# One encoder layer in float32 on one core: residual scaling on VectorE, FFN operands made operand by operand, FFN2's first casts moved

## The chip, the cores and the metric

The kernel runs on one core of one Trainium2 chip. The metric is device time in microseconds (us), the median of several runs. A profiled execution has a time of its own, and inside it a span from the first to the last instruction, in which all times of the trace are counted.

## The reference, cut to what matters

The model is a single encoder layer that is applied to a prompt of 512 tokens and to a sample of 256 tokens, each with the same 16 meta tokens in front. The width is 1024, all in float32.

```python
h   = layer_norm(concat(meta, x), ln_in_g, ln_in_b)
mix = concat(mla_attention(h), bidirectional_gated_delta_net(h)) @ w_out   # 8 heads each
h   = layer_norm(ALPHA * h + mix, ln1_g, ln1_b)
ff  = square(relu(h @ w_ff1)) @ w_ff2                                      # 1024 -> 4096 -> 1024
h   = layer_norm(ALPHA * h + ff, ln2_g, ln2_b)                             # meta tokens are dropped
```

The 768 real tokens are handled as six blocks of 128, in the order `TO = (4, 5, 1, 2, 0, 3)`. The first three blocks are "half 0" of the FFN's tokens and the last three are "half 1".

## The kernel before, in words

Each product of float32 matrices is made from three products. `split` (lines 210 to 213) rounds an operand to a short form on ScalarE (a cast, line 212) and takes the remainder on VectorE (a subtraction, line 213). TensorE then multiplies high by high, high by low and low by high.

The stages follow each other. The first layer norm and the projections (line 331) come first, up to about 270 us in the trace. The gated delta net then runs as a chain of small matrix steps (lines 837 to 882), and the attention is laid beside it: `scores` makes the softmax of one head (lines 954 to 987), `values` multiplies it with the value rows (989 to 1005). Behind them come the residual (1036 to 1049), the output projection in two passes (the loop at 1096), FFN1 (1147 to 1222) and FFN2 (1225 to 1295). The program is written in one order, but a planner with a simulated clock sets the order on each engine. From then on every engine works its queue strictly in that order. The manual dependencies marked `NOSYNC` are hints to the planner only, and nothing waits for them on the chip.

The residual. `acc` holds the six blocks of the normalized input. Each block is loaded again from `x` (1045) and normalized on ScalarE (1047). It is then multiplied by the gain row on GpSimd (1048), and the bias row is added on VectorE (1049). The two rows lie in `rbs` (1040 to 1042), in a pool that is opened after the memory of the delta net is given back. The load of block `ti` is placed behind the values of head `ti`.

The output projection. Pass 0 multiplies the delta net's output and pass 1 the attention's. Each pass loads four strips of `w_out` (1101), splits them, and makes 12 groups of 12 matmuls (1129). A group is drained into `acc` by VectorE (1131 or 1133). Pass 1 then normalizes the block (1136, 1137). After the third block it makes the transposed half 0 of the FFN's input (1138 to 1141).

FFN1 works on 2 by 2 blocks by Strassen and Winograd's scheme with seven products instead of eight. `pair(m)` computes two of the 32 strips of 128 FFN columns for both token halves. Its seven products (`prod`, 12 matmuls of 384 columns each) take the token operands B11, T2, B21, T1, T3, B22 and T4, in this order. B11 and B21 are half 0 itself. The others are sums of half 0 (kept as `raw0` in the first 3072 columns of the big tile `LT`) and half 1, made in the loop at 1152 to 1163. The sums of weights are made inside `pair`. The first two products of pairs 0 and 1 are made early (`ahead`, lines 1113 to 1117 and 1142 to 1144), into all four PSUM banks named `w`. The result `fo_` of a pair lies in `LT` where `raw0` lay. It is squared on ScalarE (1208, 1209) and stored to `FD`.

FFN2 loads the squares of a pair (`f_load`, 1235) and one strip of `w_ff2` (`w2_load`, 1242), splits both, and adds 18 matmuls (1275) for each of the 32 strips to six PSUM banks. This is done for half 0 and then for half 1. In its third step the second layer norm's gain and bias are put on `acc` by twelve VectorE operations (1263).

Of the kernel before, what the change touches and what calls it, by code (L numbers as in the profile page):

```python
# [5 lines left out]
F32 = mybir.dt.float32  # L6
# [7 lines left out]
P = 128  # L14
# [123 lines left out]
def body(ctx, tc, I, O):  # L138
# [898 lines left out]
    ex = ExitStack()  # L1037
    op = pool(ex, "op", 1)
    os_ = pool(ex, "os", 2)
    rbs = [os_.tile([P, D], F32, name="rb") for i in range(2)]  # L1040
    for i in range(2):
        ld(rbs[i], I["rows"][i].partition_broadcast(P))
# [11 lines left out]

    def w1_raw(m):

        o = 3 * D + m % 2 * 2 * D
        wr = LTf[:, o:o + 2 * D].rearrange("p (q k c) -> p q k c", q=4, k=HQ)
        ld(wr[:, 0:2], I["w_ff1"][m].rearrange("p (q k) c -> p q k c", q=2))
        ld(wr[:, 2:4], I["w_ff1"][m + 16].rearrange("p (q k) c -> p q k c", q=2))  # L1060
        return wr
# [3 lines left out]
        split(src, wh, wl)  # L1065
        return wh, wl

    def prod(w, n, ps=None):
        ps = ps if ps is not None else nbank()
        (wh, wl), (bh, bl) = w, fq[n]  # L1070
        for k in range(HQ):
            for i, (a, b) in enumerate(((wh, bh), (wh, bl), (wl, bh))):
                T.matmul(ps[:, :HR], lhsT=a[:, k, :], rhs=b[:, k, :],  # L1073
                         start=(k == 0 and i == 0), stop=(k == HQ - 1 and i == 2))
        return ps[:, :HR]

    nb = [0]
# [18 lines left out]
    for half in range(2):  # L1096
        wo = []
        for k in range(4):
            wr = op.tile([P, D], F32, name="wor", bufs=2)
            r0 = (1 - half) * 512 + k * P  # L1100
            ld(wr, I["w_out"][r0:r0 + P, :])
            wo.append([op.tile([P, D], F32R, name=n, bufs=5) for n in ("woh", "wol")])
            split(wr, *wo[k])
        if half == 1:
            banks_set(w=4, b=4)
            e5.close()
            eh = ExitStack()
# [5 lines left out]
            ahead = {}  # L1113
            for m in range(2):
                wr = LTf[:, 6 * D:7 * D].rearrange("p (q k c) -> p q k c", q=2, k=HQ)
                ld(wr, I["w_ff1"][m].rearrange("p (q k) c -> p q k c", q=2))
                ahead[m] = [w1_split(wr[:, i]) for i in range(2)]
        src = (Oa, mf)[half]
        for ti, t in enumerate(TO):
            qs = slice(t * P, t * P + P)  # L1120
            a = acc[:, ti]
            mh, ml_ = (os_.tile([P, 4, P], F32R, name=n) for n in ("mh", "ml"))
            split(src[:, :, qs], mh, ml_)
            for s in range(2):
                cs = slice(s * 512, s * 512 + 512)
                ps = bank()
                for k in range(4):
                    for i, (x, y) in enumerate(((mh, wo[k][0]), (mh, wo[k][1]), (ml_, wo[k][0]))):
                        T.matmul(ps, lhsT=x[:, k, :], rhs=y[:, cs], start=(k == 0 and i == 0), stop=(k == 3 and i == 2))  # L1129
# [19 lines left out]
    for n in ("T2", "T1", "T3", "B22", "T4"):  # L1149
        fq[n] = [hq.tile([P, HQ, HR], F32R, name=n + x) for x in "hl"]  # L1150
    fu = pool(eq, "fu", 2)
    for k in range(HQ):
# [12 lines left out]
    FD = dp.tile([16, P, 4, HR], F32, name="FD")  # L1165

    def pair(m):

        wr = w1_raw(m)
# [7 lines left out]
        sm1 = fv.tile([P, 2, HQ, P], F32, name="s12", bufs=2)  # L1177
        i1 = V.tensor_add(sm1[:, 0], wr[:, 2], wr[:, 3])
        if m in ahead:
            tc.add_manual_dep(i1.ins, normed.ins.name, NOSYNC, reason="behind the norms")  # L1180
        V.tensor_sub(sm1[:, 1], sm1[:, 0], wr[:, 0])
        p6 = prod(w1_split(sm1[:, 1]), "T2")
# [7 lines left out]
        p5 = prod(w1_split(sm1[:, 0]), "T1")  # L1190
        u4 = fu.tile([P, HR], F32, name="p5s")
        V.tensor_add(u4, u2, p5)
        yield
        V.tensor_sub(wr[:, 2], wr[:, 0], wr[:, 2])
        p7 = prod(w1_split(wr[:, 2]), "T3")
# [4 lines left out]
        V.tensor_sub(wr[:, 1], wr[:, 1], sm1[:, 1])  # L1200
        p3 = prod(w1_split(wr[:, 1]), "B22")
        V.tensor_add(fo_[:, 1], u4, p3)
        yield
        p4 = prod(w1_split(wr[:, 3]), "T4")
# [5 lines left out]
        st(FD[m], fo_)  # L1210

    for m in range(14):
        for _ in pair(m):
# [26 lines left out]
        return f[:, 0], f[:, 1]  # L1240

    def w2_load(n, ft):
        o = (3 + n % 4) * D
        wr = LTf[:, o:o + D]
        ld(wr, I["w_ff2"][ft * P:(ft + 1) * P, :])
        w = fw.tile([P, 2, D], F32R, name="w2h", bufs=7)
        return split(wr, w[:, 0], w[:, 1]), w[:, 0], w[:, 1]

    rb2 = None
    seq = [(m, i) for m in range(16) for i in range(2)]  # L1250
    for s in range(2):
# [2 lines left out]
        last = []  # L1254
        for n, (m, i) in enumerate(seq):
            if i == 0:
                fh, fl = f_load(s, m)
            x, wh, wl = w2_load(n, m + 16 * i)
            if s == 0 and n == 2:
                rb2 = rows2(2)  # L1260
                for ti in range(6):
                    for j, fn in enumerate((V.tensor_mul, V.tensor_add)):
                        y = fn(acc[:, ti], acc[:, ti], rb2[:, j])
                        tc.add_manual_dep(y.ins, x.ins.name, NOSYNC, reason="not before it is needed")
                rb2 = rows2(4)
# [46 lines left out]
```

## Time and profile before

| what | value |
|---|---|
| time, median of 3 runs | 1221.97 us (1216.72 to 1222.62) |
| the profiled execution, its own time | 1223.56 us |
| its span | 1221.8 us |
| TensorE matmuls, busy share of the span | 92% |
| VectorE, busy share | 68% |
| ScalarE, busy share | 49% |
| GpSimd, busy share | 14% |
| mean granted TensorE clock | 0.959 of full |

TensorE has the largest share by far, so the time that can be won lies where TensorE stands still or runs at a lower clock. The profile names an engine's idle time together with the instruction that ended it. The granted clock is 1.00 at 2.4 GHz and 0.50 at 1.2 GHz, and a figure between the two is a stretch that has some of each.

### The profile page before, as it was taken

What the parts mean: (1) busy time and instruction counts of PE and PEld (TensorE: products, weight loads), DVE (VectorE), ACT (ScalarE), POOL (GpSimd) and SP (SyncE); (2) the same over time, 40 slices, a digit from 0 to 9 for tenths busy, and PEclk for the clock granted to TensorE, in tenths of its full rate; (3) what the DMA queues carried; (4) which work ended last, traced back from release to release, by engine and by line L of the source; (5) the groups of instructions that cost most, each with busy time, mean ns of one, the idle gap of its engine ahead of it and who ended that gap; (6) DMA issues with size and microseconds to landing.
All of it is one profiled execution on the core that took longest, in us unless ns stands there. A gap on an engine that the chain in (4) does not pass through costs nothing.

```text
span 1221.8 us, 18631 instructions
## 1 busy us (share of the span) xinstructions
PE 1129.0 (92%) x7116; PEld 976.4 (80%) x7116; DVE 835.5 (68%) x1352; ACT 594.8 (49%) x1054; POOL 171.7 (14%) x201
## 2 busy tenths in 40 slices
PE   5978989998999999996898979999997999999997
PEld 4867879998899876663576769999997788888886
DVE  8557668688876877679646698677675844494446
ACT  5574655234745667563424566545554333333330
POOL 2144553014322211004000000000000000000000
PEclk9988899999999999897999889999999899999999
DMA  5157765532388755324102024333325765556531
GB/s 205 52 118 178 186 168 134 124 102 78 121 273 229 223 144 145 88 69 139 60 18 73 32 69 168 133 121 121 122 112 178 260 221 167 183 196 216 165 104 52
DMA packets 108107, 169.47 MB, mean 139 GB/s; under 512 B 36258, under 2 KB 72866, under 8 KB 108018
## 3 DMA queue, kind: packets, MB, share of 16 engines
q1 hardware_dynamic: 108018, 168.28, 45.0%
q8 instruction: 56, 0.92, 0.3%
q14 instruction: 33, 0.27, 0.1%
HBM read 129.14 MB, written 39.11 MB: 138 GB/s over the span
## 4 chain that ended last, share of the span: by engine, by line
PE 72%; DVE 14%; DMA 6%; issue 3%; ACT 3%; POOL 1%; SPq 1%; DVEq 0%; ACTq 0%; POOLq 0%
PE w L1275 14%; PE w L1073 9%; PE b L1073 8%; PE b L1275 7%; PE d L331 7%; PE b L1129 5%; DMA x<-gD 4%; PE c L1003 3%; PE d L972 3%; PE d L704 2%; PE b L837 2%; PE b L853 2%; PE b L877 2%; PE b L870 2%; DVE LP L598 2%
## 5 line engine op out<-in xcount | busy, mean ns | idle before, releaser
L1275 PE MATMUL w<-w2h,fh 128*128 128x512 f32 x768 | 186.9, 394 | 9.0 <-ACT fh L212 6.5
L1275 PEld LDWEIGHTS w<-w2h,fh 128*128 128x128 f32 x768 | 146.0, 190 | 40.2 <-ACT fh L212 6.8
L331 PE MATMUL d<-hTh,wl 128*128 128x384 f32 (+1 forms) x352 | 123.9, 352 | 4.4 <-DVE wl L213 4.4
L331 PE MATMUL d<-hTh,wh 128*128 128x384 f32 (+1 forms) x352 | 124.7, 354 | 1.4 <-ACT ks L188 1.4
L331 PE MATMUL d<-hTl,wh 128*128 128x384 f32 (+1 forms) x352 | 124.6, 354 | 0.0
L213 DVE TENSOR_TENSOR w2h<-LT,w2h 128x1024 fp32r<-128x1024 f32 x64 | 77.8, 1224 | 52.2 <-ACT w2h L212 50.0
L212 ACT CAST w2h<-LT 128x1024 fp32r<-128x1024 f32 x64 | 66.7, 1049 | 69.4 <-PE w L1275 27.1
L1275 PE MATMUL b<-w2h,fh 128*128 128x512 f32 x384 | 97.4, 392 | 0.0
L1275 PEld LDWEIGHTS b<-w2h,fh 128*128 128x128 f32 x384 | 72.9, 190 | 15.3
L212 ACT CAST w1h<-LT 128x512 fp32r<-128x512 f32 x80 | 49.0, 616 | 52.7 <-PE w L1073 22.6
L331 PEld LDWEIGHTS d<-hTh,wl 128*128 128x128 f32 x352 | 67.4, 192 | 6.8 <-DVE wl L213 4.7
L331 PEld LDWEIGHTS d<-hTh,wh 128*128 128x128 f32 x352 | 67.4, 191 | 5.7 <-issue 2.8
L213 DVE TENSOR_TENSOR fh<-fr,fh 128x768 fp32r<-128x768 f32 x32 | 30.5, 957 | 59.7 <-ACT fh L212 59.7
L331 PEld LDWEIGHTS d<-hTl,wh 128*128 128x128 f32 x352 | 67.3, 191 | 2.1 <-issue 1.5
L212 ACT CAST fh<-fr 128x768 fp32r<-128x768 f32 x32 | 26.7, 838 | 75.9 <-PE w L1275 38.7
L213 DVE TENSOR_TENSOR w1l<-LT,w1h 128x512 fp32r<-128x512 f32 x80 | 55.0, 688 | 5.6 <-ACT w1h L212 5.3
L1208 ACT ACTIVATE LT<-LT 128x384 f32<-128x384 f32 (+1 forms) x32 | 27.1, 846 | 46.6 <-DVE LT L1205 37.4
L972 PE MATMUL d<-kt,q 128*128 128x512 f32 (+1 forms) x96 | 46.0, 584 | 2.2 <-ACT p L188 1.3
L1003 PE MATMUL c<-pt,vt 128*64 128x512 f32 (+3 forms) x96 | 42.0, 536 | 2.6 <-ACT pt L1002 1.6
L1129 PE MATMUL b<-woh,mh 128*128 128x512 f32 x96 | 41.1, 438 | 2.3 <-DVE acc L1131 1.0
L1129 PE MATMUL b<-wol,mh 128*128 128x512 f32 x96 | 39.7, 414 | 2.4 <-DVE wol L213 2.3
L857 DVE TENSOR_TENSOR YZ<-U,b 64x512 f32<-64x512 f32 x52 | 35.5, 683 | 8.1 <-PE b L853 7.6
(455 smaller groups left out, 2789.6 us busy)
## 6 DMA issues: line engine op xcount, KB each, us to landing
LT<-in_w_ff SPq DMA_DIRECT2D x98, 512.0 KB, 4.2
FD<-LT SPq DMA_DIRECT2D x16, 768.0 KB, 3.2
fr<-FD SPq DMA_DIRECT2D x32, 384.0 KB, 3.5
wr<-in_w_in SPq DMA_DIRECT2D x22, 512.0 KB, 3.4
x<-gD SPq DMA_DIRECT2D x16, 560.0 KB, 6.0
KV<-vD SPq DMA_DIRECT2D x26, 256.0 KB, 4.3
U<-UD SPq DMA_DIRECT2D x26, 256.0 KB, 4.6
UD<-ua SPq DMA_DIRECT2D x16, 256.0 KB, 5.2
```

The lines of the kernel that those rows point to most:

```text
L212: S.copy(hi, src)
L213: return (eng or V).tensor_sub(lo, src, hi.bitcast(F32))
L331: T.matmul(ps[:, s, :c1 - c0], lhsT=a[:, k, :], rhs=b[:, k, c0:c1], start=(k == 0 and i == 0), stop=(k == KT - 1 and i == 2))
L598: V.tensor_add(Lq[:, :, i + 1:32, 0:i], Lq[:, :, i + 1:32, 0:i], tv)
L704: T.matmul(ps[:, s, :HR], lhsT=a[:, k], rhs=b[:, cs], start=(k == 0 and i == 0), stop=(k == 2 and i == 2))
L857: V.tensor_sub(YZ[h][rows], U[rows, :, :, 0], wv[rows])
L972: T.matmul(ps[:, :w], lhsT=q[:, qs], rhs=kt[:, k0:k0 + w], start=True, stop=True)
L1003: T.matmul(po[:m, :nq], lhsT=Vs[j][:, t0 + bi, :m], rhs=pt[:, :nq], start=(bi == 0), stop=(bi == ntl - 1))
L1073: T.matmul(ps[:, :HR], lhsT=a[:, k, :], rhs=b[:, k, :], start=(k == 0 and i == 0), stop=(k == HQ - 1 and i == 2))
L1129: T.matmul(ps, lhsT=x[:, k, :], rhs=y[:, cs], start=(k == 0 and i == 0), stop=(k == 3 and i == 2))
L1208: S.activation(f, f, AF.Relu)
L1275: T.matmul(po[g][h], lhsT=a[:, i_, qs], rhs=b[:, cs], start=(n_ == 0 and j == 0), stop=(n_ == len(seq) - 1 and j == 2))
```

## The change

The diff has four parts. The two rows of the residual get a pool of their own that is opened in front of the attention, the multiplication goes from GpSimd to VectorE, and the load of each block is placed one head later. The weights of pair 0 get a tile of their own (`w1x`), and all their sums and splits are made during the projection's second pass; the raw weights of FFN1 now rotate over three places. The products made ahead are placed behind the last matmul of the projection, and the token operands are made one operand after the other (T2 for all four strips, then T1, T3, B22 and T4), with sums in place in `raw0`. The last squares of pairs 14 and 15 are placed behind FFN2's first two `f_load` and first four `w2_load`, and the twelve operations on `acc` are spread over steps 8 to 13 of FFN2.

```diff
     acc = rest.tile([P, 6, D], F32, name="acc")
+    er = ExitStack()
+    rbp = pool(er, "rbp", 1, "left")
+    rbs = [rbp.tile([P, D], F32, name=f"rb{i}") for i in range(2)]
+    for i in range(2):
+        ld(rbs[i], I["rows"][i].partition_broadcast(P))
...
-        tc.add_manual_dep(i.ins, after[(0, 1, 2, 3, 4, 5)[ti]].ins.name, NOSYNC, reason="not before it is needed")
+        tc.add_manual_dep(i.ins, after[ti + 1].ins.name, NOSYNC, reason="not before it is needed")
         S.activation(a, a, AF.Identity, bias=stat[:, 1 + t, 0:1], scale=stat[:, 1 + t, 1:2])
-        G.tensor_mul(a, a, rbs[0])
+        V.tensor_mul(a, a, rbs[0])
         V.tensor_add(a, a, rbs[1])
...
-        o = 3 * D + m % 2 * 2 * D
-        wr = LTf[:, o:o + 2 * D].rearrange("p (q k c) -> p q k c", q=4, k=HQ)
+        wr = w1x if m % 3 == 0 else LTf[:, 7 * D - m % 3 * 2 * D:9 * D - m % 3 * 2 * D]
+        wr = wr.rearrange("p (q k c) -> p q k c", q=4, k=HQ)
...
+    def w1_sums(wr):
+        s12 = fv.tile([P, 2, HQ, P], F32, name="s12", bufs=2)
+        i1 = V.tensor_add(s12[:, 0], wr[:, 2], wr[:, 3])
+        V.tensor_sub(s12[:, 1], s12[:, 0], wr[:, 0])
+        V.tensor_sub(wr[:, 2], wr[:, 0], wr[:, 2])
+        V.tensor_sub(wr[:, 1], wr[:, 1], s12[:, 1])
+        return s12, i1
...
-            for m in range(2):
-                wr = LTf[:, 6 * D:7 * D].rearrange("p (q k c) -> p q k c", q=2, k=HQ)
-                ld(wr, I["w_ff1"][m].rearrange("p (q k) c -> p q k c", q=2))
-                ahead[m] = [w1_split(wr[:, i]) for i in range(2)]
+            w1x = fv.tile([P, 2 * D], F32, name="w1x", bufs=1)
+            wr0 = w1_raw(0)
+            ahead = {0: [w1_split(wr0[:, i]) for i in range(2)]}
+            wr = LTf[:, 6 * D:7 * D].rearrange("p (q k c) -> p q k c", q=2, k=HQ)
+            ld(wr, I["w_ff1"][1].rearrange("p (q k) c -> p q k c", q=2))
+            ahead[1] = [w1_split(wr[:, i]) for i in range(2)]
+            sums0 = w1_sums(wr0)
+            early = [w1_split(x) for x in (sums0[0][:, 1], sums0[0][:, 0], wr0[:, 2], wr0[:, 1], wr0[:, 3])]
...
-                        w[:] = [prod(x, n, bank("w")) for x, n in zip(w, ("B11", "B21"))]
+                        w[:] = [prod(x, n, bank("w"), outp) for x, n in zip(w, ("B11", "B21"))]
...
     for k in range(HQ):
-        b12, b22 = (h1_full(1, k + HQ * i, fu.tile([P, HR], F32, name=n)) for i, n in enumerate(("p5s", "b22")))
-        split(b22, *(x[:, k] for x in fq["B22"]))
-        t1, t2 = (fu.tile([P, HR], F32, name=n) for n in ("u2", "u3"))
-        V.tensor_sub(t1, b12, raw0(k))
-        V.tensor_sub(b12, b22, b12)
-        V.tensor_sub(t2, b22, t1)
+        ...
+        h1_full(1, k, b12)
+        h1_full(1, k + HQ, b22)
+        V.tensor_sub(raw0(k), b12, raw0(k))
+        V.tensor_sub(t2, b22, raw0(k))
         split(t2, *(x[:, k] for x in fq["T2"]))
-        split(t1, *(x[:, k] for x in fq["T1"]))
-        split(b12, *(x[:, k] for x in fq["T3"]))
-        V.tensor_sub(t2, t2, raw0(k + HQ))
-        split(t2, *(x[:, k] for x in fq["T4"]))
+    for k in range(HQ):
+        split(raw0(k), *(x[:, k] for x in fq["T1"]))
+    for k in range(HQ):
+        V.tensor_sub(b12s[k], b22s[k], b12s[k])
+        split(b12s[k], *(x[:, k] for x in fq["T3"]))
+    for k in range(HQ):
+        split(b22s[k], *(x[:, k] for x in fq["B22"]))
+    for k in range(HQ):
+        V.tensor_sub(t2s[k], t2s[k], raw0(k + HQ))
+        split(t2s[k], *(x[:, k] for x in fq["T4"]))
...
-        for q in ((0, 1), (1, 4)):
-            f = fo_[:, q[0]:q[1]]
-            S.activation(f, f, AF.Relu)
-            S.activation(f, f, AF.Square)
+        act2(fo_[:, 0:1])
+        yield
+        act2(fo_[:, 1:4])
         st(FD[m], fo_)
...
-        o = (3 + n % 4) * D
+        o = (5, 6, 3, 4)[n % 4] * D
...
+    first = [f_load(0, 0), f_load(0, 1)]
+    firstw = [w2_load(n, n // 2 + 16 * (n % 2)) for n in range(4)]
+    behind[0] = firstw[3][0]
+    for g_ in two:
+        next(g_, None)
...
-            if s == 0 and n == 2:
-                rb2 = rows2(2)
-                for ti in range(6):
-                    for j, fn in enumerate((V.tensor_mul, V.tensor_add)):
-                        y = fn(acc[:, ti], acc[:, ti], rb2[:, j])
+            if s == 0 and 8 <= n < 14:
+                if n == 8:
+                    rb2 = rows2(2)
+                for j, fn in enumerate((V.tensor_mul, V.tensor_add)):
+                    y = fn(acc[:, n - 8], acc[:, n - 8], rb2[:, j])
```

## Rows read from the trace of the kernel before

**Rows 1.** Busy time by stretch: start:end, length, then each engine; granted clock, DMA.

```profile
500.00:548.00 48.00, 46.49 (x332) 31.38 (x332) 32.34 (x83) 27.95 (x68) 0.35 (x1) 0.93 0.23 72
...
552.00:570.00 18.00, 13.57 (x36) 8.04 (x36) 17.90 (x17) 4.64 (x7) 12.89 (x5) 0.55 0.30 109
...
939.00:960.80 21.80, 12.76 (x39) 9.74 (x38) 20.29 (x19) 13.48 (x14) 0.00 (x0) 0.77 0.68 241
690.60:735.00 44.40, 34.67 (x188) 32.05 (x187) 43.31 (x86) 28.58 (x57) 0.00 (x0) 0.92 0.17 55
548.00:600.00 52.00, 38.72 (x134) 24.30 (x133) 45.39 (x68) 21.94 (x48) 15.43 (x6) 0.80 0.36 122
```

**Rows 2.** The chain of waits: start us, us, what held it.

```profile
547.94 3.83 DMA rb<-in_rows
...
551.84 2.64 POOL acc L1048
...
554.52 3.39 DVE acc L1049
...
675.80 0.69 PE w L1073
...
681.42 1.06 PE w L1073 x6
...
973.02 2.72 PE w L1275 x12
```

**Rows 3.** TensorE in order of time, where it had stood idle.

```profile
552.42 2.05 PE L896 MATMUL b<-sq,cst 128*128 128x512 f32 x2 [3.20 <-DVE sq L893]
...
707.13 0.69 PE L1073 MATMUL w<-T2h,w1h 128*128 128x384 f32 x1 [3.33 <-ACT T2h L212]
...
945.71 3.78 PE L1275 MATMUL w<-w2h,fh 128*128 128x512 f32 x8 [6.52 <-ACT fh L212]
```

**Rows 4.** ScalarE in order of time.

```profile
704.95 0.48 ACT L1175 COPY LT<-w 128x384 f32<-128x384 f32 x1
...
937.74 1.17 ACT L1208 ACTIVATE LT<-LT 128x1152 f32<-128x1152 f32 x1 [13.47 <-DVE LT L1205]
```

**Rows 5.** GpSimd and VectorE in order of time: start us, us, instruction [idle before].

```profile
551.84 13.05 POOL L1048 TENSOR_TENSOR acc<-acc,rb 128x1024 f32<-128x1024 f32 x5 [51.49 <-DMA rb<-in_rows]
...
552.19 2.40 DVE L979 SCALAR_TENSOR_TENSOR LT<-sm__5648,mx 128x96 f32<-128x96 f32 x1
...
560.40 6.09 DVE L985 TENSOR_SCALAR p<-p,rs 128x512 f32<-128x512 f32 x6
...
566.58 1.21 DVE L1049 TENSOR_TENSOR acc<-acc,rb 128x1024 f32<-128x1024 f32 x1
...
585.28 0.26 DVE L979 SCALAR_TENSOR_TENSOR LT<-sm__5783,mx 128x96 f32<-128x96 f32 x1
...
609.17 2.20 DVE L985 TENSOR_SCALAR p<-p,rs 128x512 f32<-128x512 f32 x6
```

**Rows 6.** SyncE's queue of transfers in order of time.

```profile
568.96 14.42 SPq L1101 DMA_DIRECT2D wor<-in_w_out  x5
...
624.20 16.65 SPq L1116 DMA_DIRECT2D LT<-in_w_ff  x2
...
915.45 6.59 SPq L1245 DMA_DIRECT2D LT<-in_w_ff  x4
922.09 2.76 SPq L1237 DMA_DIRECT2D fr<-FD  x2
```

**Rows 7.** Line 1047 on ScalarE: its idle time until the block's load had landed (us, times).

```profile
  DMA acc<-in_x: 7.3, 4
```

**Rows 8.** The page's costliest groups: busy, mean ns of one | idle before them.

```profile
L212 ACT CAST w2h<-LT 128x1024 fp32r<-128x1024 f32 x64 | 66.7, 1049 | 69.4 <-PE w L1275 27.1
...
L212 ACT CAST fh<-fr 128x768 fp32r<-128x768 f32 x32 | 26.7, 838 | 75.9 <-PE w L1275 38.7
L213 DVE TENSOR_TENSOR w1l<-LT,w1h 128x512 fp32r<-128x512 f32 x80 | 55.0, 688 | 5.6 <-ACT w1h L212 5.3
```

More of the change, by code (lines that the diff above doesn't have):

```diff
@@ L1039, in body @@
     os_ = pool(ex, "os", 2)
-    rbs = [os_.tile([P, D], F32, name="rb") for i in range(2)]
-    for i in range(2):
-        ld(rbs[i], I["rows"][i].partition_broadcast(P))
     for ti, t in enumerate(TO):
@@ L1066, in w1_split, with prod @@
         return wh, wl
-    def prod(w, n, ps=None):
+    def w1_sums(wr):
[5 more added lines that the diff above has]
+        return s12, i1
+    def prod(w, n, ps=None, behind=None):
         ps = ps if ps is not None else nbank()
@@ L1072, in prod @@
             for i, (a, b) in enumerate(((wh, bh), (wh, bl), (wl, bh))):
-                T.matmul(ps[:, :HR], lhsT=a[:, k, :], rhs=b[:, k, :],
-                         start=(k == 0 and i == 0), stop=(k == HQ - 1 and i == 2))
+                x = T.matmul(ps[:, :HR], lhsT=a[:, k, :], rhs=b[:, k, :],
+                             start=(k == 0 and i == 0), stop=(k == HQ - 1 and i == 2))
+                if behind is not None and k == 0 and i == 0:
+                    tc.add_manual_dep(x.ins, behind.ins.name, NOSYNC, reason="behind the projection")
         return ps[:, :HR]
@@ L1106, in body @@
             e5.close()
+            er.close()
             eh = ExitStack()
@@ L1112, in body @@
             fv = pool(ef, "fv", 2, "left")
-            ahead = {}
-            for m in range(2):
-                wr = LTf[:, 6 * D:7 * D].rearrange("p (q k c) -> p q k c", q=2, k=HQ)
-                ld(wr, I["w_ff1"][m].rearrange("p (q k) c -> p q k c", q=2))
-                ahead[m] = [w1_split(wr[:, i]) for i in range(2)]
+            w1x = fv.tile([P, 2 * D], F32, name="w1x", bufs=1)
[6 more added lines that the diff above has]
+            early = [w1_split(x) for x in (sums0[0][:, 1], sums0[0][:, 0], wr0[:, 2], wr0[:, 1], wr0[:, 3])]
         src = (Oa, mf)[half]
@@ L1128, in body @@
                     for i, (x, y) in enumerate(((mh, wo[k][0]), (mh, wo[k][1]), (ml_, wo[k][0]))):
-                        T.matmul(ps, lhsT=x[:, k, :], rhs=y[:, cs], start=(k == 0 and i == 0), stop=(k == 3 and i == 2))
+                        outp = T.matmul(ps, lhsT=x[:, k, :], rhs=y[:, cs], start=(k == 0 and i == 0), stop=(k == 3 and i == 2))
                 if half == 0:
@@ L1176, in pair @@
         yield
[L1177 to L1182, printed above, removed]
+        if m == 0:
+            w6, w5, w7, w3, w4 = early
+        else:
+            s12 = fv.tile([P, 2, HQ, P], F32, name="s12", bufs=2)
+            V.tensor_add(s12[:, 0], wr[:, 2], wr[:, 3])
+            V.tensor_sub(s12[:, 1], s12[:, 0], wr[:, 0])
+            w6 = w1_split(s12[:, 1])
+        p6 = prod(w6, "T2")
         u2 = fu.tile([P, HR], F32, name="u2")
@@ L1189, in pair @@
         yield
-        p5 = prod(w1_split(sm1[:, 0]), "T1")
+        if m:
+            w5 = w1_split(s12[:, 0])
+        p5 = prod(w5, "T1")
         u4 = fu.tile([P, HR], F32, name="p5s")
@@ L1193, in pair @@
         yield
-        V.tensor_sub(wr[:, 2], wr[:, 0], wr[:, 2])
-        p7 = prod(w1_split(wr[:, 2]), "T3")
+        if m:
+            V.tensor_sub(wr[:, 2], wr[:, 0], wr[:, 2])
+            w7 = w1_split(wr[:, 2])
+        p7 = prod(w7, "T3")
         u3 = fu.tile([P, HR], F32, name="u3")
@@ L1199, in pair, with act2 @@
         yield
-        V.tensor_sub(wr[:, 1], wr[:, 1], sm1[:, 1])
-        p3 = prod(w1_split(wr[:, 1]), "B22")
+        if m:
+            V.tensor_sub(wr[:, 1], wr[:, 1], s12[:, 1])
+            w3 = w1_split(wr[:, 1])
+        p3 = prod(w3, "B22")
         V.tensor_add(fo_[:, 1], u4, p3)
         yield
-        p4 = prod(w1_split(wr[:, 3]), "T4")
+        if m:
+            w4 = w1_split(wr[:, 3])
+        p4 = prod(w4, "T4")
         V.tensor_sub(fo_[:, 2], u3, p4)
-        for q in ((0, 1), (1, 4)):
-            f = fo_[:, q[0]:q[1]]
-            S.activation(f, f, AF.Relu)
-            S.activation(f, f, AF.Square)
+        act2(fo_[:, 0:1])
+        yield
+        act2(fo_[:, 1:4])
         st(FD[m], fo_)
+    behind = [None]
+    def act2(f):
+        x = S.activation(f, f, AF.Relu)
+        if behind[0] is not None:
+            tc.add_manual_dep(x.ins, behind[0].ins.name, NOSYNC, reason="behind the first casts")
+        S.activation(f, f, AF.Square)
     for m in range(14):
@@ L1256, in body @@
             if i == 0:
-                fh, fl = f_load(s, m)
-            x, wh, wl = w2_load(n, m + 16 * i)
-            if s == 0 and n == 2:
-                rb2 = rows2(2)
-                for ti in range(6):
-                    for j, fn in enumerate((V.tensor_mul, V.tensor_add)):
-                        y = fn(acc[:, ti], acc[:, ti], rb2[:, j])
-                        tc.add_manual_dep(y.ins, x.ins.name, NOSYNC, reason="not before it is needed")
-                rb2 = rows2(4)
+                fh, fl = first[m] if s == 0 and m < 2 else f_load(s, m)
+            x, wh, wl = firstw[n] if s == 0 and n < 4 else w2_load(n, m + 16 * i)
+            if s == 0 and 8 <= n < 14:
[3 more added lines that the diff above has]
+                    y = fn(acc[:, n - 8], acc[:, n - 8], rb2[:, j])
+                    tc.add_manual_dep(y.ins, x.ins.name, NOSYNC, reason="not before it is needed")
+                if n == 13:
+                    rb2 = rows2(4)
             last.append((n, i, fh, fl, wh, wl))
```

9 lines of the change are left out of this document (8 added, 1 removed).

## The prediction

> **What bounds the kernel now.** I read the page's busy shares first. TensorE is busy for 92% of the span, so no other engine can be the bound as a whole, and what can be won are the stretches in which TensorE stands still or runs at its lower clock. I then cut the span into stretches of 50 us with the view of busy time by stretch, looked for low TensorE time and low granted clock, and cut finer around the three places that the diff touches. The reader is to see two columns in [rows 1]: TensorE's busy time against the length, and the clock. Where TensorE is busy at the 1.2 GHz level, half of that busy time is lost as well.
>
> The three losses are these. From 548 to 600 TensorE is busy 38.7 of 52.0 us, so 13.3 are idle; from 552 to 570 the granted clock is 0.55, so about 90% of that stretch is at the lower level, and of 13.6 us of matmuls about 6.1 are lost [rows 1]. That makes 19.4 us. From 690.6 to 735.0 it is idle for 9.7 us, and a clock of 0.92 (16% at the lower level) costs 34.7 x 0.16 / 2 = 2.8; that makes 12.5 us. From 939.0 to 960.8 TensorE does 36 matmuls of FFN2 (the other three of 39 end FFN1), which cost 0.227 us each in the steady state (2.72 us for 12) [rows 2], so 8.2 us of work take 21.8 and 13.6 us are lost. The three add up to 45.5 us; no more than that is at stake.
>
> Then I asked who holds TensorE in each place, with the chain of waits and the engines in order of time. In the first, the chain goes from the gain rows' load (3.83 us) to the first GpSimd multiplication (2.64) and to VectorE's addition (3.39) [rows 2]. In the second, VectorE is busy for 43.3 of 44.4 us [rows 1] and TensorE waits 3.33 us for T2 [rows 3]. In the third, ScalarE had been idle for 13.47 us before it squared the last pairs [rows 4], and TensorE waited 6.52 us for a cast that stood behind the squares [rows 3].
>
> **Part 1, the residual.** Removed are six GpSimd multiplications; five of them run from 551.8 to 564.9 [rows 5]. While they run, VectorE's instructions are stretched: a 128x96 operation takes 2.40 us where the same line takes 0.26 later, six softmax scalings take 6.09 where they take 2.20 later, and the first addition takes 3.39 [rows 2] where a later one takes 1.21 [rows 5]. These alone are 2.1 + 3.9 + 2.2 = 8.2 us. Behind them in VectorE's queue stand the remainders of `w_out`, and the two raw buffers of `w_out` come free only with them, so five loads are spread over 14.42 us [rows 6] and the projection can't fill TensorE's idle time. With the rows in a pool that is free before the attention, the wait for their load goes too.
>
> Added are six multiplications on VectorE at the 1.21 us of the addition, which has the same shape and operands [rows 5], 7.3 us. Four blocks should now be finished under the delta net, so eight VectorE instructions or 9.7 us come into a stretch where TensorE is busy 46.5 of 48 us and VectorE 32.3 [rows 1]. The cover is VectorE's idle 15.7 us; if none of it fits, the 9.7 show in full, and since less is queued later it could also be below nothing. I take 2. There is a new wait: the multiplication waits for ScalarE, which waited 7.3 us in four times for the block's load [rows 7]. Behind it in VectorE's queue stand the drains of the delta net and the attention, and TensorE waits for those. This is priced among the rivals.
>
> What is late next in 548 to 600: the 3.2 us for the delta net's last norm [rows 3] stay, and the projection has a single PSUM bank there, so a group's drain is not hidden behind the next group. I let 13 of the 19.4 us come back. Part 1 is worth -13 + 2 = **-11** (between -19.4 and, with nothing won and 9.7 lost, +9.7).
>
> **Parts 2 and 3, FFN1's start.** The products made ahead stood in the middle of the projection with 0.69 and 1.06 us [rows 2]. Moved behind it, they let the last block be normalized 1.7 us earlier, and they cover that norm. Four sums and five remainders of pair 0 (nine VectorE instructions at 0.69 [rows 8], 6.2 us) and five casts leave the stretch from 690.6, which VectorE fills. Its subtractions and remainders for the token operands stay the same in number; only T2 comes first. So I expect 6.2 + 1.7 = 7.9 us less, minus about 0.4 for what stays late: T4 is now the last operand, and VectorE still sets when it comes.
>
> The price is paid in the projection's second pass, where those nine instructions and five casts now stand among the splits of `w_out`, and SyncE's queue, which was already held for 16.65 us by two loads [rows 6], now waits for the attention's memory with `w1x`. It lies between nothing, or slightly below since pair 0 no longer waits for its load, and 6.2 if all nine come in front of a remainder that TensorE needs. I take 1.5, near the low end, since VectorE has gaps there. Parts 2 and 3: -7.9 + 0.4 + 1.5 = **-6** (between -12.5 and +2).
>
> The raw weights' third place and the split of the squares into two steps cost nothing: from pair 2 on TensorE has no idle time that a load could shorten, and the same instructions run.
>
> **Part 4, FFN2's start.** The four strips were requested by 922.0 and the two squares by 924.9 [rows 6], so the data is there long before 939. Four casts of 1.05 and two of 0.84 us [rows 8] are 5.9 us, and they fit into ScalarE's 13.47 idle us [rows 4]; VectorE's remainders follow each. If that cover were gone, the casts would hold the last drains for at most 5.9 us. TensorE then has four steps of 18 matmuls, 16.3 us at 0.227, in hand while the last squares are made. The twelve operations on `acc` at about 1.2 us go into six steps of 4.08 us, two each, beside two remainders; the prepared steps in front hide that. A bank that is drained late may cost 1. Of 13.6 us I let **-12.5** come back (between -13.6 and -6).
>
> **The sum.** -11 - 6 - 12.5 = -29.5. The profiled execution took 1223.6 us, of which its span is 1221.8 and 1.8 lie around it, and becomes 1194.1. It stood 1.6 above the median of the runs shown, so the forecast is **1192.5 us**. Its own range, with each part between its nearer bounds (-17 to -5, -10 to -2, -13.6 to -9), is about 1181 to 1206.
>
> **Rivals.** First, the start of FFN1 gains nothing. The four products made ahead hold all four `w` banks. Pair 0's T2 product needs one, and one comes free when the first of them is copied over `raw0`. Before, this copy was at 704.95, and T2 followed at 707.13 [rows 3, 4], so the hold is real. Now `raw0` lives until T1 is split, behind all of T2. Against it: products into `b` banks can go ahead. The 6 us are gone: 1198.5.
>
> Second, VectorE is the bound from 552 to 570, and not just stretched: it is busy 17.9 of 18.0 us [rows 1]. Then the 7.3 us of multiplications come on top and only the wait of the chain (3.83 + 2.64) goes: part 1 is +0.8, the time 1204.3. Against it stand the 8.2 us of stretching, which are no work. The Trainium skill (Perfetto Trace Analysis, Optimizing Scalar/DVE Operations) says that work may be moved from a saturated VectorE even to GpSimd, which speaks against the change, and in the same breath that the two share a read port of SBUF, so that it might not help. By the first half the time is this rival's; the trace, with 2.40 us against 0.26, is nearer to the second.
>
> Third, slower. The multiplication's wait stops VectorE under the delta net. ScalarE's 7.3 us for four blocks [rows 7] are 11 for six; with twelve operations of 1.21 these are 25.5 us in front of drains that TensorE needs. If all of it reaches TensorE, which has 1.5 us of idle time there [rows 1], and nothing comes back after 548, part 1 is +25.5 and the time 1229. It decides from the point at which no attention matmul is ready while a drain waits; TensorE's 97% under the same waits of ScalarE speak against that.
>
> Fourth, the change doesn't do what it says: the dependencies only guide the planner, and the casts stay behind the last squares. Then part 4 is nothing: 1205.
>
> **How the numbers follow.** Forecast 0.65, first rival 0.15, second 0.10, third 0.05, fourth 0.05. About 0.5%, 6.1 us, is what can be told from no change. All but the third lie below 1215.9; I leave 0.03 for two of them together near that bound: faster 0.92, same 0.03, slower 0.05. The range that leaves out the third rival and the ends of the forecast's own is 1178 to 1208.
>
> **What would show it.** Right: no six-fold softmax scaling over 2.5 us after 548 and no GpSimd work there; a clock near 1.00 from 552 to 570; the five loads of `w_out` no longer spread over 14 us; nine fewer VectorE instructions of pair 0 after the projection, and TensorE idle for 2 to 4 us there; FFN2's first matmul within 1 us of FFN1's last. Wrong: TensorE idle under the delta net, ending on an `acc` multiplication; T2's first matmul waiting for the copy of pair 0's first product; FFN2 starting on a cast. The forecast as a whole is wrong if the first stretch keeps its idle time with VectorE unstretched, for then the attention's chain, and not GpSimd, held it.

## The result and the profile after

The changed kernel takes 1202.3 us (median of four runs, 1201.4 to 1204.3), the kernel before 1221.6: a ratio of 0.985, 95% interval 0.982 to 0.988. A second set on another chip gave 0.985 (0.984 to 0.987). The profiled execution took 1201.4 us, 22.2 less than the profiled one of before. The forecast was 1192.5, with 29.5 less; its range was 1178 to 1208.

Three places gained, and where each did can be read from when a line starts for the last time. The projection's first pass ends at 635.5 us instead of 646.2 (10.7 less, forecast 11). From there FFN1's 14th product comes 3.9 us sooner (forecast 6): the projection's second pass got 2.3 longer and FFN1's start 6.2 shorter. From FFN1's last product to the 36th matmul of FFN2 it takes 13.8 us instead of 21.6 (7.8 less, forecast 12.5). FFN1 and FFN2 in between and behind take the same time as before.

The first view is busy time by stretch: start:end, length, then TensorE, its weight loads, VectorE, ScalarE, GpSimd, the granted clock, DMA share and GB/s; compare [rows 1].

```profile
410.00:420.00 10.00, 6.39 (x87) 5.72 (x85) 7.43 (x13) 5.15 (x12) 2.81 (x5) 1.00 0.98 285
420.00:430.00 10.00, 9.52 (x55) 7.57 (x57) 3.64 (x8) 2.49 (x7) 0.49 (x1) 0.66 0.74 178
500.00:540.00 40.00, 40.00 (x283) 26.42 (x282) 30.85 (x65) 23.41 (x56) 0.00 (x0) 0.98 0.23 73
544.00:558.00 14.00, 10.07 (x29) 5.56 (x30) 14.00 (x28) 8.89 (x16) 0.00 (x0) 0.88 0.54 188
558.00:574.00 16.00, 16.00 (x71) 9.23 (x71) 9.79 (x28) 8.39 (x22) 0.00 (x0) 1.00 0.29 99
635.50:650.00 14.50, 12.71 (x52) 9.28 (x50) 14.50 (x24) 7.34 (x13) 0.00 (x0) 0.95 0.33 105
682.30:720.50 38.20, 35.83 (x195) 33.49 (x195) 33.06 (x68) 23.55 (x48) 0.00 (x0) 0.96 0.17 56
924.60:938.36 13.76, 10.04 (x37) 8.15 (x38) 10.99 (x11) 13.16 (x14) 0.00 (x0) 0.88 0.78 277
```

The loss under and behind the delta net is nearly gone: no GpSimd work after 544, TensorE without idle time from 500 to 540, and a clock of 1.00 from 558 to 574. Two losses are new. From 410 to 420 TensorE is idle for 3.6 us, with the DMA engines at 0.98, and from 420 to 430 its clock is 0.66. From 635.5 to 650 VectorE is busy for every microsecond. The last stretch still has 3.7 us without TensorE.

The second view is the engines in order of time at four places: the softmax scalings and the loads of `w_out` [rows 5, 6], the first attention scores, the sums of pair 0, and FFN2's start [rows 3, 4]. A bracket is the idle time before, and what ended it.

```profile
553.67 2.19 DVE L990 TENSOR_SCALAR p<-p,rs 128x512 f32<-128x512 f32 x6
545.96 13.90 SPq L1114 DMA_DIRECT2D wor<-in_w_out  x5
551.40 1.23 DVE L213 TENSOR_TENSOR wol<-wor,woh 128x1024 fp32r<-128x1024 f32 x1
552.65 0.33 SPq L1114 DMA_DIRECT2D wor<-in_w_out  x1
...
420.48 2.71 PE L967 MATMUL d<-kt,q 128*128 128x16 f32 x12 [3.90 <-DMA KV<-vD]
...
637.80 0.69 DVE L1073 TENSOR_TENSOR s<-w1x 128x512 f32<-128x512 f32 x1
642.01 1.22 DVE L213 TENSOR_TENSOR wol<-wor,woh 128x1024 fp32r<-128x1024 f32 x1
...
909.54 1.03 ACT L212 CAST w2h<-LT 128x1024 fp32r<-128x1024 f32 x1
924.60 2.94 ACT L212 CAST w2h<-LT 128x1024 fp32r<-128x1024 f32 x3 [14.03 <-PE b L1084]
927.44 1.56 ACT L212 CAST fh<-fr 128x768 fp32r<-128x768 f32 x2
928.32 3.60 PE L1326 MATMUL w<-w2h,fh 128*128 128x512 f32 x8 [3.76 <-ACT fh L212]
```

Six scalings take 2.19 us instead of 6.09. The five loads of `w_out` begin 23.0 us sooner (545.96 against 568.96). Each still goes out when a remainder is done: the third follows the one from 551.40 to 552.63. One w2 cast runs early and the other three wait 14.03 us for FFN1's last product, although their data had been requested by 905.4 us. The first scores stand at 420.5 us; in the kernel before they stood at 407.4.

### The profile page after: what moved, and what is told of

It is laid out like the page before. It is cut to its first block, busy times and chain, and to the rows that moved or that the text cites. A ratio compares the mean times of both kernels' runs of the same rounds, so it can differ in the third digit from the quotient of the medians.

```text
span 1199.4 us, 18635 instructions
## 1 busy us (share of the span) xinstructions
PE 1123.9 (94%) x7116; PEld 974.5 (81%) x7116; DVE 831.6 (69%) x1358; ACT 598.9 (50%) x1054; POOL 156.6 (13%) x195
## 4 chain that ended last, share of the span: by engine, by line
PE 77%; DVE 9%; DMA 6%; ACT 4%; issue 2%; SPq 1%; POOL 1%; DVEq 0%; ACTq 0%; POOLq 0%
PE w L1326 15%; PE w L1084 10%; PE b L1084 9%; PE d L331 7%; PE b L1326 7%; PE b L1146 5%; PE d L977 3%; PE c L1008 3%; DMA x<-gD 3%; PE b L837 2%; PE d L704 2%; PE b L853 2%; PE v L1005 2%; PE b L877 2%; PE b L870 2%
## 5 line engine op out<-in xcount | busy, mean ns | idle before, releaser
L1326 PEld LDWEIGHTS b<-w2h,fh 128*128 128x128 f32 x384 | 72.3, 188 | 15.1
L212 ACT CAST w1h<-LT 128x512 fp32r<-128x512 f32 x50 | 30.8, 620 | 41.2 <-PE w L1084 20.9
L213 DVE TENSOR_TENSOR w1l<-LT,w1h 128x512 fp32r<-128x512 f32 x50 | 34.4, 689 | 12.6 <-ACT w1h L212 12.6
L834 ACT COPY YZ<-U 64x512 f32<-64x512 f32 x52 | 32.1, 617 | 17.3 <-issue 11.3
L978 DVE TENSOR_REDUCE mx<-d 128x1 f32<-128x512 f32 (+1 forms) x48 | 28.7, 599 | 16.7 <-PE d L977 16.5
```

What stands on the lines that cost most here:

```text
L212: S.copy(hi, src)
L213: return (eng or V).tensor_sub(lo, src, hi.bitcast(F32))
L834: S.copy(YZ[h][rows], U[rows, :, :, 1])
L978: V.tensor_reduce(mx[:, 0, t:t + 1], ps[:, :w], AX.X, ALU.max)
L1326: T.matmul(po[g][h], lhsT=a[:, i_, qs], rhs=b[:, cs], start=(n_ == 0 and j == 0), stop=(n_ == len(seq) - 1 and j == 2))
```

## The experiments

All twelve, with their places in the profiled execution, in us from the delta net's first state update (its first matmul of YZ with XAb, line 877, at 373 to 379 us of the span), so that what an execution loses before it does not enter. "First scores" is the first matmul of the attention, "pass 1" the last drain of the projection's first pass, "pass 2" the time from there to the projection's last matmul, "proj. end" that matmul, "FFN2" the time from FFN1's last product to FFN2's 36th matmul. Executions of the same code still differ by up to 3 us at pass 1. Ratios are to the kernel before on the same chip.

| kernel | mul, rows, acc loads | first scores | pass 1 | pass 2 | proj. end | FFN2 | median | ratio (95%) |
|---|---|---|---|---|---|---|---|---|
| before | GpSimd, late, early | 31.2 | 270.0 | 44.1 | 314.1 | 21.6 | 1218.0 to 1221.6 | 1 |
| changed | VectorE, early, later | 44.7 | 259.7 | 46.4 | 306.1 | 13.8 | 1202.3 | .985 (.982-.988) |
| e1 | VectorE, early, later | 44.2 | 261.5 | 45.1 | 306.6 | 21.6 | 1214.2 | .996 (.994-.998) |
| e2 | GpSimd, late, early | 31.8 | 269.5 | 41.4 | 310.9 | 21.3 | 1214.5 | .996 (.994-.998) |
| e3 | GpSimd, late, early | 31.1 | 267.3 | 43.7 | 311.0 | 13.8 | 1212.5 | .994 (.992-.997) |
| e4 | GpSimd, early, later | 44.3 | 257.8 | 45.0 | 302.8 | 13.6 | 1199.0 | .983 (.981-.986) |
| e5 | as changed | 44.0 | 260.1 | 44.3 | 304.4 | 14.8 | 1203.3 | .985 (.984-.987) |
| e6 | VectorE, late, later | 31.1 | 262.2 | 40.6 | 302.8 | 13.9 | 1199.5 | .982 (.980-.984) |
| e7 | as changed | 42.9 | 256.4 | 45.4 | 301.8 | 11.8 | 1199.2 | .981 (.978-.984) |
| e8 | as changed | 43.4 | 260.1 | 44.2 | 304.3 | 14.8 | 1203.1 | .984 (.982-.986) |
| e9 | GpSimd, late, later | 31.0 | 265.0 | 40.4 | 305.4 | 14.6 | 1200.6 | .986 (.984-.988) |
| e10 | VectorE, early on top, later | 37.9 | 255.0 | 45.1 | 300.1 | 15.1 | 1194.3 | .982 (.980-.984) |
| e11 | as e10 | 37.1 | 252.1 | 45.4 | 297.5 | 8.2 | 1189.8 | .977 (.975-.979) |
| e12 | as e10, rows behind first q | 31.0 | 251.1 | 42.0 | 293.1 | 8.2 | 1186.1 | .973 (.970-.975) |

**The parts alone (e1 to e3).** e1 is the kernel before with the hunks of the rows' pool, of the loads' dependency and of the multiplication; e2 with those of the weights and token sums; e3 with the squares, first casts and strips (taken in the order 3, 5, 4, 6).

> Only part 1 of the change (early rows, loads of acc one pass later, residual scaled on VectorE). Theory A, the parts are independent and worth what the two traces show in their stretches: 10.8 us less than before (first pass of the projection ends at 635.5 instead of 646.3), nothing given back later; the first scores matmul stands near 420 us as in after and not at 407. Rival B, the second pass or FFN1's start gives part of it back, since their loads and casts are then what is late: 5 to 8 us less. The prediction's own term was 11 us less.

> Only parts 2 and 3 (token sums operand by operand, first pair's weights early), without the residual's edit and without the edit at FFN2's start. Theory A, from the two traces: 3.6 us less than before (6.0 us less between the projection's end and the 14th product, 2.4 us more in the projection's second pass). The prediction's term: 6 us less. Rival B: before, the residual still sits on GpSimd, the second pass has other slack, and the price of 2.4 us is not paid: 6 us less with the second pass at 44.4 us.

> Only part 4 (FFN2's first casts in front of the last squares); the four raw strips of w2 are taken where the first kernel's weight strips come free. Theory A, the second cast waits for the last product on T4 because its buffer lies over T4's, whatever stands before it: 8.0 us less than before, FFN2's first matmul some 3.7 us after FFN1's last, one w2 cast before that and three behind it. Theory B (the prediction's term): four casts before FFN1's end, 12.5 us less. If the buffers were not what holds the casts but the load of the strips, the casts' idle time would name a DMA.

Each part does in its stretch what it does in the changed kernel. Part 1 ends the first pass 8.5 us sooner than before. Part 4 gives 13.8 instead of 21.6, so its buffers hold the cast whatever stands in front. Parts 2 and 3 do better alone: their second pass takes 41.4 us, less than the 44.1 before, where the changed kernel has 46.4. So the price of the second pass is paid only together with part 1 (rival B). By medians the parts are worth 3.8, 3.5 and 5.6 us, less than their profiles say (9.1, 8.7, 8.8): the profiled execution of before stands 5.5 us above the median of the 24 runs on that chip, theirs 0.3 to 2.3 above their own. The product of the three ratios, 0.987, agrees with the 0.985 of the whole within their intervals.

**Which edit of part 1 (e4 to e6, e9).** The engine and the rows are undone one at a time and together; e5 is the changed kernel on the chip of e6.

```diff
-        V.tensor_mul(a, a, rbs[0])      # e4, e9
+        G.tensor_mul(a, a, rbs[0])
...
-    rbp = pool(er, "rbp", 1, "left")    # e6, e9: rows back behind the delta net
...
+    rbs = [os_.tile([P, D], F32, name="rb") for i in range(2)]
```

> The changed kernel with one word undone: the residual is multiplied on GpSimd again, with the rows still early and the loads of acc still one pass later. Theory A, the stretched probability scalings carried part 1: over 6 of its 10.8 us are lost, scalings of some 6 us and multiplications of some 13 us are back after 544 us. Theory B, the early rows carried it: under 3 us are lost, since only the last three loads of acc fall after 544 us and the earlier multiplications lie under the delta net, where VectorE has slack.

> The changed kernel as it is, for comparison on the same chip as the next three. With the residual on GpSimd and the rows early it took 1199.0 us where the kernel before took 1218.0. If the engine of the multiplication is worth nothing (theory B after that run), this one takes 1197 to 1202; if the VectorE form is better after all, it lies 3 us or more below 1199.

> The changed kernel with only the early rows undone: the residual is multiplied on VectorE, the loads of acc come one pass later, but the two gain rows stand in the pool behind the delta net again and are loaded when it ends. Theory B, the early rows carried part 1: 7 to 12 us slower than the changed kernel, the projection's first pass ends at 643 us or later, and VectorE stands still behind the rows' load near 548. Theory A, the engine carried it (no GpSimd work, so no stretched scalings): under 4 us slower, the first pass ends before 640.

> The fourth corner of the square of engine and rows: the changed kernel with the residual on GpSimd and the rows loaded when the delta net ends, so that of part 1 only the loads of acc one pass later are left. The other corners on this scale: VectorE and early rows 1203, GpSimd and early rows 1199, VectorE and late rows 1199.5. Theory A, the harm is the meeting of both (all GpSimd multiplications pile up behind the late rows and run beside VectorE's chain), and either edit takes it away: 6 to 10 us slower than the other corners, first pass of the projection ends at 645 us or later, softmax scalings over 5 us for six are back. Rival B, the later loads of acc carried part 1: within 2 us of 1199.5, first pass by 640.

e4 says that the engine is worth nothing (.983 against .985 for e5, with intervals that overlap), e6 that the early rows, as they are placed, are worth nothing, and e9, with both undone, keeps the gain. e5 took 1.3 us more than the range expected of it. What is left in e9 is the edit that the prediction gave no price: each load of `acc` one pass of the attention later. Up to FFN1's end e9 and e2 differ in that alone, and the projection ends at 305.4 instead of 310.9. The times say the same: e2's and e3's ratios multiply to .991, and e9 has .986 (.984 to .988). From there, either of the other two edits gives 2.6 more (e4, e6), which is within the spread of single executions, and both together nothing that can be told (304.4 and 306.1). The last corner, the new engine and the early rows with the loads as before, was not run: whether those two would do it without the later loads is open. My theory before e9 (without both, the harm is back in full) fell. The GpSimd and VectorE rows of e2, then of e9, in span times, show how the loads act:

```profile
551.59 12.87 POOL L1048 TENSOR_TENSOR acc<-acc,rb 128x1024 f32<-128x1024 f32 x5 [49.09 <-DMA rb<-in_rows]
559.96 6.10 DVE L985 TENSOR_SCALAR p<-p,rs 128x512 f32<-128x512 f32 x6
574.44 1.22 DVE L1049 TENSOR_TENSOR acc<-acc,rb 128x1024 f32<-128x1024 f32 x1
584.25 0.68 DVE L1145 SCALAR_TENSOR_TENSOR acc<-acc,b 128x512 f32<-128x512 f32 x1
```

```profile
548.74 10.30 POOL L1048 TENSOR_TENSOR acc<-acc,rb 128x1024 f32<-128x1024 f32 x4 [50.51 <-DMA rb<-in_rows]
557.02 4.02 DVE L985 TENSOR_SCALAR p<-p,rs 128x512 f32<-128x512 f32 x6
566.49 1.21 DVE L1049 TENSOR_TENSOR acc<-acc,rb 128x1024 f32<-128x1024 f32 x1
577.42 0.68 DVE L1145 SCALAR_TENSOR_TENSOR acc<-acc,b 128x512 f32<-128x512 f32 x1
```

With one block fewer in front of the late rows, GpSimd's run is four long, the scalings take 4.02 us, and from the start of that run VectorE takes 17.8 us to the last addition instead of 22.9, and 28.7 to the projection's first drain instead of 32.7. In e4 the multiplications come one by one, and a multiplication stretches one product at most:

```profile
525.70 2.36 POOL L1050 TENSOR_TENSOR acc<-acc,rb 128x1024 f32<-128x1024 f32 x1 [23.38 <-ACT acc L1049]
527.17 1.43 DVE L900 TENSOR_TENSOR LT<-LT,zz 128x512 f32<-128x512 f32 x1
...
550.42 2.99 POOL L1050 TENSOR_TENSOR acc<-acc,rb 128x1024 f32<-128x1024 f32 x1 [22.36 <-ACT acc L1049]
551.22 2.73 DVE L900 TENSOR_TENSOR LT<-LT,zz 128x512 f32<-128x512 f32 x1
553.88 2.19 DVE L990 TENSOR_SCALAR p<-p,rs 128x512 f32<-128x512 f32 x6
```

The product L900 takes 2.73 and 1.43 us beside these multiplications and 0.67 to 0.69 in e4 where GpSimd is idle; the scalings behind it are at 2.19. It began 0.8 us after the one multiplication and 1.5 after the other, and both times it ended 0.54 us after the multiplication did: it looks held until GpSimd is done, and then made. Three of e4's six multiplications stretch nothing. So it is the run of GpSimd instructions beside VectorE's chain that costs, not GpSimd. The Trainium skill (SBUF — State Buffer, Who interferes with whom) has it that the two engines share a port pair, an exclusive lock; VectorE instructions with two SBUF inputs contend for it with GpSimd's reads, and so can a scaling, in a mode in which whoever issues first keeps the pair for its whole instruction and blocks the other. These rows agree: products and scalings are both stretched (2.73 against 0.67, 6.10 against 2.19), and L900 ends when GpSimd lets go.

**Where the early rows' gain went (e10, e12).** In the changed kernel the rows' pool lies in front of the attention's pools. Two things follow, read from the built programs and the queue: the attention's buffers stand 8 KB higher, over tiles that the stage before still stores from until 400 us, and its loads come later in SyncE's queue (those of `kt` from 404.0 us, before from 355.9). e10 opens the pool behind the attention's, e12 also issues the two loads behind the first head's.

```diff
-    rbp = pool(er, "rbp", 1, "left")          # in front of kp, qp, pp, tp, sm
...
     sm = pool(e5, "sm", 6, "left")
+    rbp = pool(er, "rbp", 1, "left")          # e10; with its loads
...
     prev = scores(0)
+    rbp = pool(er, "rbp", 1, "left")          # e12; with its loads
```

> The changed kernel with the pool of the early rows opened behind the attention's pools instead of in front of them, so that the attention's buffers stand at their old addresses and its loads in their old places of the queue. Theory A, the 8 KB in front pushed the attention's first loads behind the last stores of the stage before, and with them the attention's end, w1's load and the sums into the second pass: first scores matmul back from 420 to 407 us, second pass of the projection 41 to 43 us instead of 44 to 46, 3 to 5 us faster than the changed kernel. Rival B, the later attention only lets the delta net run ahead, and what it costs comes back there: first scores at 407, but the time within 1.5 us of the changed kernel's 1203.

> The run before (rows on top, FFN2's start mended) with one more edit: the loads of the two gain rows are issued behind the first attention head's loads, not in front of them. Theory A, with the buffers at their old addresses the 1 MB of rows still stood in front of vt and q in the queue, while the DMA engines were busy for 0.95 to 1.06 of the time (400 to 420 us), and that is why the first scores came at 412.6 to 416.4 and not at 407: they now stand at 406 to 409 us. If this start sets the time, 2 to 5 us less than the run before; Rival B, the rows only delay the next head's q instead, and the delta net gives the difference back: first scores at 407, the ratio within 0.2% of that run's 0.9769.

e10's ratio is 0.3 points lower than the changed kernel's (the intervals overlap), but its first scores came only half of the way back and its second pass stayed at 45.1 us: one reason was missing. The queue of e10 shows the 1 MB of rows in front of the first `q`, and e12 takes it away. SyncE and TensorE of e10, then of e12:

```profile
404.36 0.85 SPq L947 DMA_DIRECT2D rb<-in_rows  x2
408.42 0.60 SPq L962 DMA_DIRECT2D q<-QD  x1
416.39 1.51 PE L967 MATMUL d<-kt,q 128*128 128x16 f32 x12
```

```profile
399.82 0.43 SPq L957 DMA_DIRECT2D q<-QD  x1
403.05 0.85 SPq L1013 DMA_DIRECT2D rb<-in_rows  x2
404.83 1.41 PE L962 MATMUL d<-kt,q 128*128 128x16 f32 x12
```

The first scores are back at 31.0 and the projection ends at 293.1, 21.0 us sooner than before. The time is 0.4% below e11, from which e12 differs in this alone (intervals .970 to .975 and .975 to .979, which touch). Up to the projection's end e12 differs from e6 only in the early rows, and it ends 9.7 us sooner (293.1 against 302.8). By the medians I estimate 5 us: .973 against .982, less the .005 by which e11 is below e10. So the early rows do gain, once they stand in nobody's way.

**The second pass (e8).** The sums of pair 0 were written behind the second block instead of in front of the pass.

> The changed kernel with pair 0's sums, remainders and casts made after the second block of the projection's second pass instead of in front of it. Theory A, in the changed kernel these nine VectorE instructions and five casts (VectorE 15.0 of 15.0 us busy from 635 to 650) stand in front of the remainders of w_out, and that is the price of 2.4 us and more in the second pass: 2 to 4 us faster, the projection ends 2 to 4 us earlier and FFN1's start is unchanged. Rival, the second pass is held by its own loads and casts of w_out, and the sums only fill the time, or they now come in front of the norms: 0 to 2 us slower.

This one told nothing: the planner put VectorE's instructions in the same order as before, TensorE's waits in the second pass were the same, and so was the time. Where the price comes from is therefore read from traces, not tried. In e6 the attention ends earlier (last scores at 204.5 on the scale of the table, against 210.8 in e5), and with it `w1x`, which lies over its buffers, is loaded earlier (9.7 us before the last drain of the first pass, in e5 3.4). Three of the four sums and four remainders are done when the second pass begins, and it takes 40.6 us. The rows are the second pass of e6, then of e5:

```profile
638.10:679.10 41.00, 36.70 (x158) 28.47 (x159) 32.60 (x74) 20.39 (x39) 0.00 (x0) 0.96 0.16 56
```

```profile
635.70:680.40 44.70, 38.18 (x167) 29.76 (x166) 36.90 (x81) 24.39 (x46) 0.00 (x0) 0.96 0.19 64
```

Seven VectorE instructions and 4.3 us of its work stand inside the pass in e5 that were done before it in e6. They don't hold up the remainders of `w_out`: the last one starts 6.55 us after the first pass's last drain in both. They stand in front of the pass's first drain, which starts after 10.7 us in e5 and after 8.6 in e6. What TensorE waited for VectorE's drains in the pass (us, times, longest), in e6, e5 and e1:

```profile
PE b L1143 <- DVE acc L1147: 0.4, 1, 0.4
PE b L1146 <- DVE acc L1150: 2.2, 3, 1.2
PE b L1132 <- DVE acc L1136: 0.4, 1, 0.4
```

e1 has the late attention without the sums, and not the wait (its pass takes 45.1 us with the products made ahead still in it). The rest of the difference is that fewer of the pass's matmuls run before the last drain of the first: they begin 0.8 us before it in e5, 4.4 in e6. e12 has the attention on time, but its first pass ends so early that `w1x` again comes 3.4 us before that end, and the wait is there as in e5.

**FFN2's start (e7, e11).** The second to fourth w2 buffers lie over the token operands that were made last, and the one made last is T4, which FFN1's last product reads.

```diff
-    for n in ("T2", "T1", "T3", "B22", "T4"):
+    for n in ("T2", "T4", "B22", "T3", "T1"):         # e7, e11, e12
...
-        V.tensor_sub(fo_[:, 2], u3, p4)
+        lastev.append(V.tensor_sub(fo_[:, 2], u3, p4))   # e11, e12
...
+    for x in lastev[-2:]:
+        for y in (behind[0], lowf[1]):
+            tc.add_manual_dep(x.ins, y.ins.name, NOSYNC, reason="behind the first remainders")
```

> The changed kernel with the buffers of the token operands made in the order T2, T4, B22, T3, T1 instead of T2, T1, T3, B22, T4, so that the second to fourth w2 buffers of FFN2 lie over T1, T3 and the end of B22, which are read for the last time some 4 to 12 us before T4. Theory A, the buffer over T4 held the second cast and with it ScalarE's queue: the cast's wait of 14.0 us for FFN1's last product is gone, FFN2's first matmul stands within 1 us of FFN1's last, 4 to 5 us faster than the changed kernel. Rival, the remainder on VectorE or the fh casts hold it anyway: under 1.5 us.

> The run before with the token buffers in the order T2, T4, B22, T3, T1 and VectorE's last two drains of FFN1 put behind the remainders of the first four w2 strips and two token strips (behind the other order alone, those remainders still stood behind the drains, from 918.2 to 924.6 us). Theory A: FFN2's 36th matmul comes 9 to 10 us after FFN1's last product, against 13.8 in the changed kernel and 12.1 with the order of buffers alone, so 4 to 5 us faster than the run before it. Rival B, the late drains hold PSUM banks that FFN2 needs, and TensorE waits for those instead: 0 to 2 us.

In e7 the wait of 14.0 us is gone, but the time to the 36th matmul falls only to 11.8 (the rest of what e7 gained stands in the first pass, 256.4, for which I have no reason). ScalarE is done with all casts by 916; VectorE's remainders stand behind its last two drains:

```profile
913.43 1.05 ACT L212 CAST w2h<-LT 128x1024 fp32r<-128x1024 f32 x1 [3.10 <-PE b L1084]
914.38 1.56 ACT L212 CAST fh<-fr 128x768 fp32r<-128x768 f32 x2
917.76 0.56 DVE L1243 TENSOR_TENSOR LT<-u,b 128x384 f32<-128x384 f32 x1 [1.53 <-PE b L1084]
918.23 4.62 DVE L213 TENSOR_TENSOR w2h<-LT,w2h 128x1024 fp32r<-128x1024 f32 x4
919.51 1.90 PE L1326 MATMUL w<-w2h,fh 128*128 128x512 f32 x7 [1.55 <-DVE w2h L213]
```

e11 puts the drains behind them, and FFN2 follows FFN1 without a gap: 8.2 us for 36 matmuls, what they cost in the steady state.

```profile
912.00 4.62 DVE L213 TENSOR_TENSOR w2h<-LT,w2h 128x1024 fp32r<-128x1024 f32 x4
916.54 1.82 DVE L213 TENSOR_TENSOR fh<-fr,fh 128x768 fp32r<-128x768 f32 x2
918.28 0.55 DVE L1243 TENSOR_TENSOR LT<-u,w 128x384 f32<-128x384 f32 x1
915.49 1.53 PE L1329 MATMUL w<-w2h,fh 128*128 128x512 f32 x6
```

The late drains held nothing up, so rival B is out. e12, which joins all of this, beats both kernels: 1186.1 us, a ratio of 0.973.

## Why the prediction was right, and where it was not

**Part 1** was right in size in the two profiled executions (10.7 of 11; alone, by the medians of e1, it is worth 3.8), and in its signs for the end state: no GpSimd work, scalings at 2.19 us, a clock of 1.00 from 558 to 574. It was wrong in what brings it there, so that 10.7 met 11 is luck in part. The step "while they run, VectorE's instructions are stretched" holds, but the prediction let the new engine and the early rows take the run away; as they are placed, the two together add nothing to the later loads (ratio .986 without them, .985 with them), for which the prediction had no term. The term of 2 under the delta net was also another thing than the prediction said. No multiplication stopped VectorE there. Instead the step "the rows in a pool that is free before the attention" has a price that I left out: the pool's place and its loads push the attention's start back by 13 us. The delta net runs ahead meanwhile and ends at 163.4 on the table's scale instead of 171.5, so the first pass still looks as forecast. Without that price the first pass ends at 251.1 (e12), 18.9 less than before, close to the 19.4 that [rows 1] put at stake. The sign "the five loads no longer over 14 us" failed: 13.90. What the prediction said of these loads holds even so. Each goes out when a remainder frees a buffer, and the five are nearly as far apart as before (14.42), but they begin 23.0 us sooner, and the sign should have been that.

**Parts 2 and 3** brought 6.2 us at FFN1's start and cost 2.3 in the second pass, net 3.9 of 6. The first term was forecast as 7.5 net, and TensorE's idle time of 2.4 us there is in the range that was named. The price of 1.5 was too low only in company: alone (e2) the second pass gained 2.7. And it is paid at the projection's drains, not, as the prediction had it, at the remainders. The rival in which pair 0's T2 waits for a `w` bank did not come: its product went into a `b` bank, from 697.2 us.

**Part 4** is the term that was mis-sized, 7.8 for 12.5. "The data is there long before" was true, and it wasn't enough: a cast also needs the place that it writes, which the last product was still reading, and ScalarE takes its queue in order, so two strips and both token casts stood behind it. Of the 5.6 us that were still to be had (13.8 against 8.2 in e11), the buffers' order gave back 2.0 to 3.0 (e7 against the changed kernel and e5) and VectorE's order the other 3.6 (e11).

**The base.** The terms were taken from one profiled execution, which I set 1.6 us above the median. On the chip of the result it is 2.0 above the median of the four runs, and 5.5 above that of the 24 runs on another chip, so some 0.4 to 4 us more of what lay in that trace may not have been there to be won from a median. In which stretch this lies is open: e2 and e3, which share the way to the end of the first pass with the kernel before, end it at 269.5 and 267.3 against 270.0.

## What to carry to other kernels

When work is moved ahead of its old place, look at three things besides its data: the buffer that it writes and who still reads what lies there, the place of its loads in the transfer queue, and which drains stand in front of it on each engine it uses. A pool that is opened in front of others moves all of their buffers; open it behind them. And when a part has several edits, price each one alone: here the smallest, a dependency shifted by one pass, was enough for what the other two were credited with, and the early rows showed a gain of their own only when they were moved out of the attention's way.

## What was not expected of the hardware

A GpSimd multiplication of 2.3 to 3.0 us stretches one VectorE product to 2.73 us at most (0.67 alone) when it comes singly, and six scalings to 4.02 or 6.10 (2.19 alone) when four or five follow each other. And 1 MB of loads in front of a 384 KB load, with the DMA engines at 0.95 to 1.06 busy from 410 to 420 us, put off the first matmul that needs it by 6.1 to 6.9 us (e12 against e11 and e10). Of this, 3.7 to 3.9 us are that the load was issued later, since the delta net's loads came in between; the rest is that it took longer to land.
